# TensorE held to the planner's order, and float32 steps let in by groups

## The chip, the cores and the metric

The kernel runs on one core of one Trainium2 chip. The metric is the device time of one execution in microseconds (us). The profile shows one execution, with the engines TensorE (PE, its weight loads as PEld), VectorE (DVE), ScalarE (ACT), GpSimd (POOL) and SyncE (SP).

## The reference, cut to what matters

Two transformer blocks on 256 tokens of width 1024, in float32:

```python
def first_block(x, mem, ...):                 # two layers
    for l in range(2):
        if l == 1: k_shared, v_shared = split(rmsnorm(h, kv_norm) @ w_kv)
        main, mq = split(rmsnorm(h, norm_mix[l]) @ w_in[l])
        main_out = pool_mixer(main) if l == 0 else swa_sink_attention(norm(main), k_shared, v_shared, sinks)
        mem_out = memory_attention(norm(mq), mk, mv)        # mk, mv = mem @ w_mem_kv[l]
        h = h + concat(main_out, mem_out) @ w_out[l]
        h = h + relu(rmsnorm(h) @ w_up[l])**2 @ w_down[l]
def second_block(x, ...):
    hq, hf, hi, hg, aq, ak, av, gl = split(rmsnorm(x) @ w_in)
    y_hg = hgrn2_mix(hq, hf, hi, hg) @ w_branch_hg          # a gated linear recurrence, 8 heads
    att = moba_attention(norm(aq), norm(ak), av, bias)      # 256 tokens: causal softmax attention, 8 heads of 128
    x = x + (sigmoid(gl0) * y_hg + sigmoid(gl1) * (att @ w_branch_attn)) @ w_out
    return x + (silu(rmsnorm(x) @ w_gate) * (rmsnorm(x) @ w_up)) @ w_down
```

## The kernel before, in words

All large products are made of split operands. An activation x is kept as xh + xl and a weight as wh + wl, both halves in float32r, and each product is three matmuls (xh wh, xh wl, xl wh) into one PSUM bank. `lin` (L316) has 128 tokens as the stationary operand and 512 weight columns moving; `lin_T` (L327) has 128 weight columns stationary and 256 tokens moving. Weights stream in through the SP queue in units of two k-tiles (`load_units`, L227), and ACT and DVE make wh and wl of each. These products are the long steps here.

The rest of TensorE's work is short and in plain float32: transposes (`tr`, L158), scores, values, the pooling products and the products of the recurrence. In the trace a plain float32 matmul stands as two instructions, a transpose as one. A stage has four PSUM banks for `acc` and four for `mm`.

The order of the program is written by a planner, `Line` (L84). Each piece of work is a generator with a rank. A `yield` of a number says how long after now its next step is due; a `yield` of events waits until all are due; `Event.at(lat)` sets a due time. `mm` and `tr` move the planner's clock `now` by the time that they are taken to need. `run` (L105) takes, of all steps that are due, the one with the lowest rank. `lin` yields after every six matmuls and `lin_T` after every twelve, so that short steps can come between. Within one step nothing comes between.

What the planner writes is the program order. In the first section (L727 to L827) DVE, ACT, POOL and PE keep it. Behind that section the compiler's scheduler puts each engine's instructions in order when it builds the program: it goes by priority (the program order), models when operands will be ready, and takes a later instruction where an earlier one would have to wait.

Three stages mix short chains with long products:

- the first mixing stage (about 42 to 84 us): `pool_mix` (rank 4, L911), `mem_attention` for two token tiles (ranks 3 and 4, L861), against the second memory projection (rank 14) and `mixer_out` (ranks 20 and 21);
- the second (about 300 to 353 us): four `swa` chains (ranks 4 and 7, two at a time by `slots`, L1004), two `mem_attention` chains (ranks 3 and 6), against `in_proj` (ranks 12 and 17) and `mixer_out`;
- the third (about 550 to 800 us): `diagonal` and `recurrence` (ranks 5, 8, 9), `heads_T` (rank 9), two `attend` chains (ranks 4 and 5, L1396), against `attention_in` (rank 10) and `sides` (rank 12).

Two places hold two results in one PSUM bank and read the first before they write the second:

```python
# attend, score(hp): one acc bank for two heads                       L1407
for i in range(2):
    mm(ps[:, i, :nk], aq[tt][:, hd, :], ak[hd // 4][:, hd % 4, :nk])
    V.tensor_tensor_reduce(sc[:, i, :nk], ps[:, i, :nk], ...)
# pool_mix: one mm bank for tiles k0 and k0 + 1, three banks           L931
for k in (k0, k0 + 1):
    ... mm(ps[q0:q1, k - k0, :], pw[...], u[...], ...)
    A.activation(xh, ps[:, k - k0, :], AF.Copy, ...)
    V.scalar_tensor_tensor(xl, ps[:, k - k0, :], ..., xh, ...)
```

`swa` takes a bank for each head, and `mem_attention` issues all its score matmuls before the first read.

Of the kernel before, what the change touches and what calls it, by code (L numbers as in the profile page):

```python
# [9 lines left out]
F32R = mybir.dt.float32r  # L10
# [9 lines left out]
TT = S // P  # L20
# [21 lines left out]
def kernel(  # L42
# [8 lines left out]
    nc = tc.nc  # L51
    V, A, G, PE = nc.vector, nc.scalar, nc.gpsimd, nc.tensor

    const = ctx.enter_context(tc.tile_pool(name="const", bufs=1))
    wpool = ctx.enter_context(tc.tile_pool(name="wpool", bufs=1))
    keep = ctx.enter_context(tc.tile_pool(name="keep", bufs=1))
# [19 lines left out]
    class Event:  # L76


        t = None
# [4 lines left out]
    class Line:  # L84

        def __init__(self):
            self.now = 0.0  # L90
            self.tasks = []

        def add(self, rank, gen):
            t = [rank, 0.0, gen, None]
            self.tasks.append(t)
            return t

        def start_of(self, t):
# [6 lines left out]
        def run(self, until):  # L105
            left = list(until)
            while any(t in self.tasks for t in left):
                can = [(t, self.start_of(t)) for t in self.tasks]
                can = [(t, s) for t, s in can if s is not None]
                first = min(s for _, s in can)  # L110
                self.now = max(self.now, first)
                t = min((t for t, s in can if s <= self.now), key=lambda t: t[0])
                try:
                    y = next(t[2])
                except StopIteration:
                    self.tasks.remove(t)
                    continue
                if isinstance(y, (int, float)):
                    t[1] = self.now + y
                else:  # L120
                    t[3] = [y] if isinstance(y, Event) else list(y)

    line = Line()
# [26 lines left out]

    def mm(out_, lhsT, rhs, start=True, stop=True):
        PE.matmul(out_, lhsT, rhs, start=start, stop=stop)  # L152
        n = math.prod(rhs.shape[1:])
        m = math.prod(lhsT.shape[1:])
        side_by_side = 4 if m <= 32 else 2 if m <= 64 else 1
        line.now += max(n, min(m, 64)) / 2400.0 * (1 if rhs.dtype == F32R else 4) / side_by_side + 0.0025

    def tr(out_, in_):  # L158
        PE.transpose(out_, in_, ident)  # L159
        line.now += 0.109  # L160

    def acc_bank():
# [373 lines left out]
    def mixer_out(key, xs, cuts, there):  # L536

        left = {(tt, c): len(cuts) + 1 for tt in range(TT) for c in range(2)}

        def task(tt, k0, k1, wait):  # L540
            yield wait
            for c in range(2):
                acc = acc_bank()
                yield from lin(acc, ktiles(xs, tt)[k0:k1], W((key, k0, c)))
                left[tt, c] -= 1
                residual_ms(tt, c, acc, left[tt, c] == 0)

        return [line.add(20 + tt, task(tt, k0, k1, wait)) for tt in range(TT)
                for k0, k1, wait in zip((0,) + cuts, cuts + (KT,), there[tt])]


# [171 lines left out]
        V.tensor_sub(xs[1][:, o, :], r, xs[0][:, o, :].bitcast(F32))  # L723

    pw = act.tile([P, 6, 192], F32, tag="pw", name="pw")
    ET = mybir.EngineType
    with tc.manual_schedule(engines={ET.DVE, ET.Activation, ET.Pool, ET.PE}):  # L727

        x_raw, m_raw = raw_T(), raw_T()

        warm = mm_bank()
        for _ in range(12):
            PE.matmul(warm[:, :P], ones, ones, start=True, stop=True)

        def units_of(i, **a):
            key, w = plan[i][:2]
            ready[key] = []
            units = load_units(*w, **a)

            def more():  # L740
                ready[key] += next(units)
                return ready[key][-KU:], len(ready[key]) - KU

            return more

        def columns_T(ps, xs, w, k, c0):

            for i, (wh, wl) in enumerate(w):
                xh, xl = ktiles(xs)[k + i]
                c = slice(c0, c0 + P)  # L750
                for j, (a, b) in enumerate(((wh, xh), (wh, xl), (wl, xh))):
                    mm(ps, a[:, c], b, k + i + j == 0, k + i == KT - 1 and j == 2)

        def rows(accs, xs, w, k):
            for tt in range(TT):
                run(lin(accs[tt], ktiles(xs, tt)[k:k + KU], w, k == 0, k + KU == KT))

        load_T(x_raw, xT, 0, 2)
        ups = [acc_bank()[:, :S] for _ in range(4)]
        more = units_of(0, apart=1)  # L760
        for k in range(0, KT, KU):
            if k:
                load_T(x_raw, xT, k, 2)
            split_raw(x_raw, xs0, k, 2, G_MIX)
            w, _ = more()
            for i in range(4):
                columns_T(ups[i], xs0, w, k, i * P)
        ups += [mm_bank()[:, :S] for _ in range(2)]
        more = units_of(1)
        pool_short()  # L770
        ws = []
        for k in range(0, KT, KU):
            w, _ = more()
            ws += w
            for i in range(2):
                columns_T(ups[4 + i], xs0, w, k, i * P)
        for tt in range(TT):
            nc.sync.dma_start(h[tt], x[0, tok(tt), :])
        nc.sync.dma_start(cols, columns)
        for k in range(0, KT, 4):  # L780
            load_T(m_raw, memT, k, 4)

        dg = act.tile([P, TT, P], F32, tag="dg", name="dg")
        nx = [Norm(h[tt]) for tt in range(TT)]
        for tt in range(TT):
            for c in range(2):
                nx[tt].add(c)
            x_r[tt] = nx[tt].rstd()
            V.tensor_scalar(dg[:, tt, :], ident, x_r[tt], None, op0=ALU.mult)
        split_raw(m_raw, mem_set, 0, 4)  # L790
        qs = mm_bank().rearrange("p (t c) -> p t c", t=TT)
        rb = act.tile([P, S], F32, tag="rb", name="rb")
        more = units_of(2)

        def queries(tt):
            run(lin(qs[:, tt, :], ktiles(xs0, tt), [(wh[:, 256:], wl[:, 256:]) for wh, wl in ws]))

        queries(0)
        ps = mm_bank()[:, :S]
        for tt in range(TT):  # L800
            PE.matmul(ps[:, tok(tt)], ones, dg[:, tt, :], start=True, stop=True)
        A.copy(rb, ps)
        queries(1)
        for i in range(2):
            V.tensor_tensor(u[:, i, :], ups[i], rb, ALU.mult)
        w, k = more()
        accs1 = [acc_bank() for _ in range(2)]
        rows(accs1, mem_set, w, k)
        split_raw(m_raw, mem_set, 4, 4)
        for i in range(2, 4):  # L810
            V.tensor_tensor(u[:, i, :], ups[i], rb, ALU.mult)
        rows(accs1, mem_set, *more())
        for i in range(4, 6):
            V.tensor_tensor(u[:, i, :], ups[i], rb, ALU.mult)
        for tt in range(TT):
            A.activation(mq[tt], qs[:, tt, :], AF.Copy, scale=x_r[tt])
        m = [act.tile([P, D], F32, tag="raw_T", name="mem", bufs=4) for _ in range(TT)]
        tc.keep_in_program_order(nc.sync.dma_start(m[0], mem[0, tok(0), :]))
        rows(accs1, mem_set, *more())
        tc.keep_in_program_order(nc.sync.dma_start(m[1], mem[0, tok(1), :]))  # L820
        mem_r[0] = row_norm(m[0])
        rows(accs1, mem_set, *more())
        mem_r[1] = row_norm(m[1])
        nc.gpsimd.dma_start(pw, pool_w[0].rearrange("g a d -> (g a) d").rearrange("(j p) d -> p j d", p=P))
        for e in mem_there:
            e.at()
# [6 lines left out]
    def add_mem_kv(l, rank, lat, accs=None):  # L833
# [10 lines left out]
                A.activation(v[:, mt, :], acc[:, 256:], AF.Copy, scale=mem_r[mt])  # L844
                key_tasks.append(line.add(3, keys_T(acc, mem_r[mt], kT, mt, there[mt], lat)))

        return kT, v, there, line.add(rank, proj())

    def keys_T(acc, r, kT, tt, done, lat):

# [139 lines left out]

    act.open("mlp0")
    new_h()
    t = line.add(26, mlp("mlp0", xs, there, 8, 4, SqRelu(), residual_r))
    xs1 = xset()
    there1 = add_turned(xs1)
    line.run([t, t_bias])
# [86 lines left out]
        line.add(4, keys_T(acc, h_r[tt], skT, tt, sk_there[tt], 6.0))  # L1083

    for tt in range(TT):
        line.add(9, kv_proj(tt))
        line.add(12, in_proj("in1", 0, xs1, tt, h_r, pj, there1[tt]))
    for tt in range(TT):
        line.add(17, in_proj("in1", 1, xs1, tt, h_r, pj, there1[tt]))
    mts = xset()  # L1090
    mixed, recalled = [events() for _ in range(2)], events()

# [60 lines left out]

    t_line = line.add(2, bias_line())
    new_h()
    t = line.add(11, mlp("mlp1", xs, there, 8, 4, SqRelu(), residual_2))
    x2 = xset()
    there2, = add_norms((x2, gain(G_MIX2)))
    line.run([t, t_line])
# [154 lines left out]
                yield from to_tm("hi", c, hv, tt)  # L1314
            hv_there[tt].at(3.2)

    line.add(3, values_h())
    for c in range(2):
        line.add(3, gates_T(c))
        line.add(8 + c, recurrence(c))  # L1320


# [129 lines left out]
        done.at(3.0)  # L1452

    yat, yat_there = xset(), events()
    line.add(10, attention_in())
    for tt in range(TT):
        line.add(4 + tt, attend(tt, yat, yat_there[tt]))

# [58 lines left out]
                        residual(tt, c, accs[c])  # L1517

    new_h()
    t = line.add(12, sides())  # L1520
    xs = xset()
    there, = add_norms((xs, gain(G_FFN)))
    line.run([t])
# [8 lines left out]
        if last:  # L1532
            nc.sync.dma_start(out[0, tok(tt), cs], hs)

    line.run([line.add(26, mlp("ffn", xs, there, 11, 2, SiluGate(), finish, 2))])
    act.close()


# [49 lines left out]
```

## Time and profile before

| | |
|---|---|
| median of 3 runs | 1039.11 us (1039.04 to 1039.41) |
| the profiled execution | 1038.09 us, its span 1036.1 us |
| PE busy | 1025.5 us (99%) |
| DVE, ACT, POOL busy | 639.7 (62%), 562.8 (54%), 99.1 us (10%) |
| chain that ended last | PE 96% |

The span is from the first to the last instruction of the execution. The ends of matmuls are modelled, so that starts are read, not ends; two starts in a row give what the first one cost.

### The profile page before, as it was taken

To read this page: it belongs to the slowest core of one execution; us is meant where nothing else is said; L and a number is where in the kernel's file an instruction comes from. 1 tells how busy PE (TensorE), PEld (TensorE's weight loads), DVE (VectorE), ACT (ScalarE), POOL (GpSimd) and SP (SyncE) were. 2 spreads that over 40 slices of the span, in tenths; PEclk is the share of its full clock that TensorE was granted. 3 is DMA by queue.
4 is the path that set the end of the run, shared out by engine and by line. 5 is a ranking of instruction groups with operands and counts; after the bars stand their busy time and mean duration, and the time that the engine had idled before them with its cause. 6 is when DMAs were issued, how large, how long until landed. Compare 5 with 4: busy or idle time off the path is not lost.

```text
span 1036.1 us, 18404 instructions
## 1 busy us (share of the span) xinstructions
PE 1025.5 (99%) x7352; PEld 904.8 (87%) x7352; DVE 639.7 (62%) x1001; ACT 562.8 (54%) x901; POOL 99.1 (10%) x143
## 2 busy tenths in 40 slices
PE   8999999999999999999999999999999999999998
PEld 8768989998876788899988988888999988999997
DVE  5886655556668666464576569847635766464552
ACT  6775554454678654454465444758644555344351
POOL 1515000000143000000000004330000000000000
PEclk9999999999999999999999999999999999999999
DMA  9754556546642258656557544344365566565741
GB/s 320 269 181 136 181 184 211 191 163 204 202 164 82 57 189 317 210 185 213 173 182 235 193 165 153 119 137 145 119 203 180 169 196 210 164 211 164 234 144 41
DMA packets 107749, 186.40 MB, mean 180 GB/s; under 512 B 6792, under 2 KB 31632, under 8 KB 107664
## 3 DMA queue, kind: packets, MB, share of 16 engines
q1 hardware_dynamic: 106560, 180.43, 53.4%
q0 software_dynamic: 1104, 4.80, 1.4%
q8 instruction: 57, 0.93, 0.4%
q14 instruction: 28, 0.23, 0.1%
HBM read 182.58 MB, written 2.63 MB: 179 GB/s over the span
## 4 chain that ended last, share of the span: by engine, by line
PE 96%; DVE 1%; POOL 1%; DMA 1%; ACT 0%; issue 0%; SPq 0%; ACTq 0%
PE acc L152 59%; PE mm L152 33%; PE mm L159 3%; DMA raw<-in_w_in_dram 1%; POOL win L921 0%; DVE wl L251 0%; DVE wl L246 0%; POOL st L419 0%; POOL win L920 0%; POOL st L348 0%; ACT wh L250 0%; DVE win L921 0%; ACT wh L245 0%; ACT xh L722 0%; SPq L235 0%
## 5 line engine op out<-in xcount | busy, mean ns | idle before, releaser
L246 DVE TENSOR_TENSOR wl<-raw,wh 128x1024 fp32r<-128x1024 f32 (+1 forms) x315 | 378.1, 1223 | 172.2 <-ACT wh L245 165.6
L245 ACT CAST wh<-raw 128x1024 fp32r<-128x1024 f32 (+1 forms) x315 | 322.3, 1047 | 170.7 <-PE acc L152 101.8
L152 PE MATMUL mm<-xh,wh 128*128 128x256 f32 x752 | 208.4, 277 | 0.0
L152 PE MATMUL mm<-xl,wh 128*128 128x256 f32 x752 | 208.0, 277 | 0.0
L152 PE MATMUL mm<-xh,wl 128*128 128x256 f32 x752 | 207.9, 277 | 0.0
L152 PEld LDWEIGHTS mm<-xh,wh 128*128 128x128 f32 x752 | 141.2, 188 | 1.4 <-issue 0.4
L152 PEld LDWEIGHTS mm<-xl,wh 128*128 128x128 f32 x752 | 141.3, 188 | 1.0
L152 PEld LDWEIGHTS mm<-xh,wl 128*128 128x128 f32 x752 | 141.3, 188 | 0.0
L152 PE MATMUL acc<-wh,xh 128*128 128x512 f32 x336 | 138.3, 412 | 1.2 <-ACT wh L250 1.2
L152 PE MATMUL acc<-wh,yl 128*128 128x512 f32 x342 | 134.8, 394 | 0.0
L152 PE MATMUL acc<-wl,yh 128*128 128x512 f32 x342 | 134.0, 392 | 0.0
L152 PE MATMUL acc<-wl,xh 128*128 128x512 f32 x336 | 132.4, 394 | 1.1 <-DVE wl L251 1.1
L152 PE MATMUL acc<-wh,yh 128*128 128x512 f32 x342 | 133.4, 390 | 0.0
L152 PE MATMUL acc<-wh,xl 128*128 128x512 f32 x336 | 132.6, 395 | 0.0
L152 PE MATMUL acc<-xh,wh 128*128 128x256 f32 x416 | 117.1, 281 | 1.0 <-ACT wh L245 1.0
L152 PE MATMUL acc<-xh,wl 128*128 128x256 f32 x416 | 116.5, 280 | 1.2 <-DVE wl L246 1.2
L152 PE MATMUL acc<-xl,wh 128*128 128x256 f32 x416 | 116.2, 279 | 0.0
L152 PEld LDWEIGHTS acc<-xh,wl 128*128 128x128 f32 x416 | 78.7, 189 | 1.8 <-DVE wl L246 1.8
L152 PEld LDWEIGHTS acc<-xh,wh 128*128 128x128 f32 x416 | 78.6, 189 | 1.6 <-ACT wh L245 1.6
L152 PEld LDWEIGHTS acc<-xl,wh 128*128 128x128 f32 x416 | 78.2, 188 | 0.0
L152 PEld LDWEIGHTS acc<-wh,xh 128*128 128x128 f32 x336 | 63.2, 188 | 16.0 <-issue 2.5
L152 PEld LDWEIGHTS acc<-wl,yh 128*128 128x128 f32 x342 | 64.2, 188 | 13.7
(240 smaller groups left out, 1277.6 us busy)
## 6 DMA issues: line engine op xcount, KB each, us to landing
raw<-in_w_in_dram SPq DMA_DIRECT2D x87, 512.0 KB, 4.7
raw<-in_w_up_dram SPq DMA_DIRECT2D x64, 512.0 KB, 4.8
raw<-in_w_down_dram SPq DMA_DIRECT2D x64, 512.0 KB, 4.8
raw<-in_w_out_dram SPq DMA_DIRECT2D x24, 512.0 KB, 4.6
raw<-in_w_ffn_gate_dram SPq DMA_DIRECT2D x44, 256.0 KB, 4.3
raw<-in_w_ffn_up_dram SPq DMA_DIRECT2D x44, 256.0 KB, 4.6
raw<-in_w_ffn_down_dram SPq DMA_DIRECT2D x22, 512.0 KB, 5.3
raw<-in_w_mem_kv_dram SPq DMA_DIRECT2D x8, 512.0 KB, 9.4
```

What stands on the lines that cost most here:

```text
L152: PE.matmul(out_, lhsT, rhs, start=start, stop=stop)
L159: PE.transpose(out_, in_, ident)
L245: A.copy(wh[:, ks, :], raw[:, ks, :])
L246: V.tensor_sub(wl[:, ks, :], raw[:, ks, :], wh[:, ks, :].bitcast(F32))
```

## The change

An outer `manual_schedule` around the whole kernel makes TensorE keep the program order everywhere; the other engines are scheduled as before. Each task is marked as long (split products) or short, and the planner gets a rule, `choose`. It knows by `in_long` whether the last matmul written was a float32r one. If it was, a short step of a rank above 2 is put off as long as a long step is due and the earliest due time among the due short steps lies less than 1.6 us back. If it was not, due short steps go ahead of a long one.

```diff
+    ET = mybir.EngineType
+    ctx.enter_context(tc.manual_schedule(engines={ET.PE}))
...
+        PATIENCE = 1.6
...
+            self.in_long = True
-        def add(self, rank, gen):
-            t = [rank, 0.0, gen, None]
+        def add(self, rank, gen, long=False):
+            t = [rank, 0.0, gen, None, long]
...
+        def choose(self, ready):
+            t, _ = min(ready, key=lambda c: c[0][0])
+            longs = [c for c in ready if c[0][4]]
+            short = [c for c in ready if not c[0][4]]
+            if not longs or not short:
+                pass
+            elif self.in_long:
+                if t[0] > 2 and not t[4] and self.now - min(s for _, s in short) < self.PATIENCE:
+                    t = min(longs, key=lambda c: c[0][0])[0]
+            elif t[4]:
+                t = min(short, key=lambda c: c[0][0])[0]
+            return t
...
-                t = min((t for t, s in can if s <= self.now), key=lambda t: t[0])
+                t = self.choose([(t, s) for t, s in can if s <= self.now])
...
         PE.matmul(out_, lhsT, rhs, start=start, stop=stop)
+        line.in_long = rhs.dtype == F32R
...
         PE.transpose(out_, in_, ident)
+        line.in_long = False
...
-        return [line.add(20 + tt, task(tt, k0, k1, wait)) for tt in range(TT)
+        return [line.add(20 + tt, task(tt, k0, k1, wait), True) for tt in range(TT)
...
-    with tc.manual_schedule(engines={ET.DVE, ET.Activation, ET.Pool, ET.PE}):
+    with tc.manual_schedule(engines={ET.DVE, ET.Activation, ET.Pool}):
...
-    line.add(10, attention_in())
+    line.add(10, attention_in(), True)
```

The same mark `True` goes to the other tasks of long products: the memory projection, `kv_proj`, both `in_proj`, the three `mlp`, `values_h`, `gates_T` and `sides`.

## Rows read from the trace of the kernel before

**Rows 1.** The page: busy time of the engines, share of span.

```profile
PE 1025.5 (99%) x7352; PEld 904.8 (87%) x7352; DVE 639.7 (62%) x1001; ACT 562.8 (54%) x901; POOL 99.1 (10%) x143
```

**Rows 2.** Busy time by stretch: two mixing stages; length, engines, granted clock, DMA.

```profile
52.90:84.00 31.10, 30.18 (x161) 19.79 (x160) 22.79 (x54) 18.72 (x44) 9.68 (x13) 1.00 0.48 150
302.60:352.80 50.20, 50.18 (x327) 34.40 (x326) 35.65 (x132) 35.78 (x106) 13.82 (x36) 1.00 0.23 71
```

**Rows 3.** Timeline of PE, second mixing stage: start, length, instruction, shape, count.

```profile
302.60 0.49 PE L159 MATMUL mm<-ident,qn 128*128 128x128 f32 x3
302.84 0.48 PE L152 MATMUL acc<-wh,xh 128*128 128x512 f32 x1
303.15 0.39 PE L152 MATMUL acc<-wl,xh 128*128 128x512 f32 x1
...
304.07 0.40 PE L152 MATMUL acc<-wh,xl 128*128 128x512 f32 x1
304.39 0.49 PE L152 MATMUL acc<-skT,qT 64*128 64x128 f32 x4
304.81 0.50 PE L152 MATMUL acc<-wh,xh 128*128 128x512 f32 x1
305.15 0.39 PE L152 MATMUL acc<-wl,xh 128*128 128x512 f32 x1
305.38 0.39 PE L152 MATMUL acc<-wh,xl 128*128 128x512 f32 x1
...
350.74 0.66 PE L152 MATMUL mm<-eT,sv 128*64 128x128 f32 x8
```

**Rows 4.** Timeline of PE and DVE, the first scores of `attend`.

```profile
705.19 0.82 PE L152 MATMUL acc<-ak,aq 128*128 128x128 f32 x4
...
705.71 0.29 DVE L1411 CUSTOM_DVE_ANT_0 sc<-acc,rel 128x128 f32<-128x128 f32 x1 [1.64 <-PE acc L152]
...
706.07 0.47 PE L152 MATMUL acc<-ak,aq 128*128 128x128 f32 x2
706.15 0.42 DVE L1411 CUSTOM_DVE_ANT_0 sc<-acc,rel 128x256 f32<-128x256 f32 x1
...
706.64 0.70 PE L152 MATMUL acc<-ak,aq 128*128 128x256 f32 x2
```

**Rows 5.** Timeline of PE and DVE, a later score of `attend`.

```profile
711.08 0.39 PE L152 MATMUL acc<-ak,aq 128*128 128x128 f32 x2
...
713.88 0.29 DVE L1411 CUSTOM_DVE_ANT_0 sc<-acc,rel 128x128 f32<-128x128 f32 x1
...
714.73 0.38 PE L152 MATMUL acc<-ak,aq 128*128 128x128 f32 x2
```

**Rows 6.** Timeline, first mixing stage: the pooling products and their readers.

```profile
53.43 1.86 PE L152 MATMUL mm<-u,pw 128*128 128x256 f32 x8
...
55.61 0.85 ACT L941 ACTIVATE xh<-mm,cols 128x256 fp32r<-128x256 f32 x2
...
58.70 1.22 PE L152 MATMUL mm<-u,pw 64*64 64x256 f32 x4 [0.92 <-DVE u L926]
...
61.35 0.48 DVE L942 SCALAR_TENSOR_TENSOR xl<-mm,cols,xh 128x256 fp32r<-128x256 f32 x1
```

**Rows 7.** Timeline of PE: memory attention's scores (mkT) and turned softmax (me).

```profile
56.08 1.13 PE L152 MATMUL acc<-mkT,mqT 64*128 64x256 f32 x8
...
68.97 0.60 PE L159 MATMUL mm<-ident,me 128*128 128x128 f32 x4
...
331.53 1.14 PE L152 MATMUL acc<-mkT,mqT 64*128 64x256 f32 x8
...
336.61 0.60 PE L159 MATMUL mm<-ident,me 128*128 128x128 f32 x4
```

**Rows 8.** Timeline: the recurrence's last products, and the first later use of their result.

```profile
682.55 0.39 PE L152 MATMUL mm<-hv,AX 128*128 128x128 f32 x2
...
713.27 0.69 DVE L1482 TENSOR_TENSOR ho<-ho,hgate 128x512 f32<-128x512 f32 x1
```

More of the change, by code (lines that the diff above doesn't have):

```diff
@@ L725 @@
     pw = act.tile([P, 6, 192], F32, tag="pw", name="pw")
-    ET = mybir.EngineType
-    with tc.manual_schedule(engines={ET.DVE, ET.Activation, ET.Pool, ET.PE}):
+    with tc.manual_schedule(engines={ET.DVE, ET.Activation, ET.Pool}):
         x_raw, m_raw = raw_T(), raw_T()
@@ L845, in proj @@
                 key_tasks.append(line.add(3, keys_T(acc, mem_r[mt], kT, mt, there[mt], lat)))
-        return kT, v, there, line.add(rank, proj())
+        return kT, v, there, line.add(rank, proj(), True)
     def keys_T(acc, r, kT, tt, done, lat):
@@ L992 @@
     new_h()
-    t = line.add(26, mlp("mlp0", xs, there, 8, 4, SqRelu(), residual_r))
+    t = line.add(26, mlp("mlp0", xs, there, 8, 4, SqRelu(), residual_r), True)
     xs1 = xset()
@@ L1085 @@
     for tt in range(TT):
-        line.add(9, kv_proj(tt))
-        line.add(12, in_proj("in1", 0, xs1, tt, h_r, pj, there1[tt]))
+        line.add(9, kv_proj(tt), True)
+        line.add(12, in_proj("in1", 0, xs1, tt, h_r, pj, there1[tt]), True)
     for tt in range(TT):
-        line.add(17, in_proj("in1", 1, xs1, tt, h_r, pj, there1[tt]))
+        line.add(17, in_proj("in1", 1, xs1, tt, h_r, pj, there1[tt]), True)
     mts = xset()
@@ L1155 @@
     new_h()
-    t = line.add(11, mlp("mlp1", xs, there, 8, 4, SqRelu(), residual_2))
+    t = line.add(11, mlp("mlp1", xs, there, 8, 4, SqRelu(), residual_2), True)
     x2 = xset()
@@ L1315, in values_h @@
             hv_there[tt].at(3.2)
-    line.add(3, values_h())
+    line.add(3, values_h(), True)
     for c in range(2):
-        line.add(3, gates_T(c))
+        line.add(3, gates_T(c), True)
         line.add(8 + c, recurrence(c))
@@ L1519 @@
     new_h()
-    t = line.add(12, sides())
+    t = line.add(12, sides(), True)
     xs = xset()
@@ L1533, in finish @@
             nc.sync.dma_start(out[0, tok(tt), cs], hs)
-    line.run([line.add(26, mlp("ffn", xs, there, 11, 2, SiluGate(), finish, 2))])
+    line.run([line.add(26, mlp("ffn", xs, there, 11, 2, SiluGate(), finish, 2), True)])
     act.close()
```

## The prediction

> **What bounds the kernel now.** The page's first part comes first: TensorE is busy 99% of the span and the next engine 62% [rows 1]. A time can thus change in three ways only: TensorE gets other matmuls (it does not, the products are the same), a matmul costs another pitch, or TensorE stands. The busy share can't show which, as the modelled ends cover short waits. So I read starts in the timeline. Two wide long matmuls in a row start 0.23 us apart (305.15, 305.38), and stretches of long products alone run at that pitch from end to end; nothing is to be had there, and the planner writes them in one order with or without the rule. What is left are the stages that mix. By the windows, two of them last 31.1 and 50.2 us [rows 2], with DVE at 73% and 71% and ACT at 60% and 71%, so that the chains compete there for DVE and ACT with the making of wh and wl.
>
> **What a change between long and short costs.** Three transposes and the long one behind them take 302.60 to 303.15, 0.55 us; less 0.23 that is 0.107 us for each transpose, and nothing for the change [rows 3]. Four score instructions on half the rows of the array (64*128) are another matter: from the last long one before (304.07) to the second behind (305.15) pass 1.08 us; less two pitches, 0.62 us. Two side-by-side pairs at 0.11 (a pair streams as many columns as a transpose) would need 0.22, so this group pays 0.40 us for changing to and fro [rows 3]. I count 15 groups with such half-array forms between long ones in the second stage, from 304.39 to 350.74 [rows 3], and take half as many, 8, in the first (an estimate). Transposes, the scores of `attend` and its values use the whole array: by the first reading they pay nothing.
>
> [...]
>
> **The change part by part.**
>
> *Grouping.* A short step is now put off by 1.6 us of planner time, and since it can enter only after a long step of six matmuls (1.3 us), by 1.6 to 2.9 us; those that fall due meanwhile go with it. Saved at most: all 15 + 8 groups at 0.40, 9.2 us; at least nothing. Chains fall due at scattered moments and at most four run at once, so I let about a third, 7.5 groups, merge: **-3 us**. In the recurrence the two halves already go together, so nothing merges there. Each of its levels becomes due some 2 us later; over seven levels the chain ends some 12 us later. What hides that: its last product starts at 682.55 and the result is first used at 713.27 [rows 8], 30 us later; beyond that margin every us would count.
>
> *Order kept: the scores of `attend`.* Before, the scheduler puts something between the two heads of one bank: the other tile's head and a long matmul. The rows show why: TensorE issues the first halves of both tiles at 705.19, DVE reads the first tile's at 705.71, and the second half starts at 706.07, right behind the read; the other tile's read starts at 706.15 and takes 0.42, and its second half starts at 706.64 [rows 4]. In program order head 0, its read and head 1 are one step, so TensorE stands in between, and the long products queue behind it. Price with DVE free: a first half of two instructions at 0.11 leaves TensorE free at 705.41, so 0.66 us until 706.07; the wider one leaves at 705.85 (two of 0.22 behind it), so 0.79 until 706.64. Two tiles by four calls: 4 x 0.66 + 4 x 0.79 = 5.8 us at least. With DVE taken by something else it is much more: at 711.08 a first half is issued, free at 711.30, but DVE reads it only at 713.88 and is done at 714.17 [rows 5], a wait of 2.9 us. Half of the calls like that and half free would make 4 x 2.9 + 4 x 0.72 = 14.5. I take six at 0.72 and two halfway (1.8): **+8 us**, nearer the lower end, because a TensorE that stands asks for fewer wh and wl meanwhile.
>
> *Order kept: `pool_mix`.* The same in three banks, with two readers in a row: the score's wait less its read, 0.66 - 0.29 = 0.37, plus ACT 0.43 (0.85 for two), plus DVE 0.48 [rows 6] and one more hand-over of 0.07 (706.00 to 706.07 in rows 4): 1.35 us a bank, 4.1 for three. Upper bound: the first half of the first bank is issued at 53.43 and its xl starts at 61.35 [rows 6], 7.9 us, because DVE makes the windows and wl first; with two free banks 10.6. Of this 0.92 is already paid (TensorE idle before 58.70 [rows 6]). Lower bound, where these waits only replace what the stage loses to DVE anyway: nothing. I take 4.1 + 1 for DVE's queue - 0.9: **+4 us**.
>
> *Order kept: the softmax of `mem_attention`.* The planner makes its transposes due 3.2 us behind the scores. The trace has 12.9 us (56.08 to 68.97) in the first stage and 5.1 (331.53 to 336.61) in the second [rows 7]. With patience the distance becomes 4.8 to 6.1. In the second stage that is enough; in the first up to 12.9 - 4.8 = 8 us can be exposed, once, though much of that distance is TensorE's own pooling work. Between 0 and 8: **+2 us**.
>
> *Long work used up.* Long steps that go ahead of due shorts in the second stage are missing later, when only chains are left. The half of `in_proj` that fills there is 48 matmuls, 11 us. If it ends early, TensorE stands in the gaps of two chains at a time; I bound this by 0 and 6 (about half the filler) and take **+1 us**.
>
> Nothing moves on the SP or POOL queues; no DMA is issued by TensorE. The first section already kept this order.
>
> Sum: -3 + 8 + 4 + 2 + 1 = +12 us. Against the profiled execution, 1038.09 us (1036.1 span and 2.0 around it), that is 1050; the median of the runs is 1.0 higher, so 1051.
>
> **The rivals.**
>
> *Not slower: grouping outweighs the waits.* The place is the two mixing stages. It decides where merged groups x 0.40 exceed the new waits. If nearly all 23 merge (-9.2) and the first stage is bound by DVE in either order (pooling and softmax waits 0), what stays is the scores' 5.8: -3.4, 1035.7. For it: DVE at 73% in that stretch, and a wait already there. Against: 5.8 comes from rows with DVE free, and chains of seven steps can't all fall together. Chance 0.14.
>
> *No change that shows.* Merges save 8 or so and only the floor of the waits is paid, within 2 us of zero: 1039. It needs the planner's due times to lie behind the real ones nearly everywhere, as they do where stages are calm. Chance 0.13.
>
> *Waits compound.* If the planner is early throughout, each stall delays the reads behind it and the stage goes at the pace of the chains: scores 14.5, pooling 9.7, softmax 8, filler 6, grouping -3, +35 at the top; halfway between that and the forecast is +23, 1062. For it: the distances of rows 5 to 7. Against: in those the scheduler had given DVE other work because nothing pressed. Chance 0.20.
>
> *The forecast.* Chance 0.53, with its own range of 1044 to 1058 (scores 6 to 11, pooling 1 to 7, the rest as above).
>
> **How the numbers follow.** 0.2% is 2 us, about what a measurement can tell here. Faster by more: 0.14 from the first rival. Same: 0.13. Slower: 0.53 + 0.20 = 0.73. The range leaves out most of the first rival below and the upper half of the third above, 0.1 each: 1037 to 1064.
>
> **What the profile after would show.** Right: the two heads' instructions of one tile stand next to each other in `attend`, with PE starts 0.9 us or more apart and waits of PE on DVE L1411 in the view of waits, eight of them, 6 to 11 us in all, between about 700 and 760; waits of PE on DVE L942 in the first mixing stage; fewer groups of half-array forms in the second (about 10 for 15), each longer; long stretches as before at 0.23. Wrong: no PE wait on L1411, or the third stage no longer than now; the second stage shortened by more than 5 us (grouping worth more than I give it); or the time moved in a stretch of long products, where I see nothing to move.

## The result, and the profile after

The changed kernel takes 1068.68 us (median of 4 runs, 1067.32 to 1070.12), the kernel before 1039.22 beside it: a ratio of 1.0283 [1.0267, 1.0299], 29.5 us slower. Slower was forecast, by 12 us; the time lies above the range that went up to 1064.

First the page of the kernel after: busy time by engine, TensorE's granted clock over 40 slices of the span, and the chain that ended last. They answer to [rows 1].

```profile
PE 1030.0 (97%) x7352; PEld 908.6 (85%) x7352; DVE 642.7 (60%) x1001; ACT 564.0 (53%) x901; POOL 103.4 (10%) x143
...
PEclk9989999999998999999999999999899999999999
...
PE 92%; DVE 3%; ACT 2%; issue 1%; DMA 1%; POOL 1%; SPq 0%; DVEq 0%; ACTq 0%
```

The instruction counts are the same, and the busy share is again useless: it fell by two points for 29.8 us of span. What is new is that the chain leaves TensorE for DVE and ACT, and that three slices of the clock read 8. So the next view is the one of waits (engine and line that waited, what for; us in total, times, longest).

```profile
PE acc L173 <- DVE s L1433: 9.4, 8, 5.2
PE mm L173 <- DVE xl L964: 7.7, 3, 5.5
PE mm L173 <- ACT eT L471: 3.6, 3, 2.3
PE acc L173 <- ACT qT L1044: 3.6, 1, 3.6
```

L1433, L964 and L173 are L1411, L942 and L152 of the kernel before. None of these four rows is in its view of waits. The eight waits of the first row are the scores of `attend`, the three of the second the pooling, and the four of the last two rows belong to the short chains, three of them in the second stage.

Where the time went is read from landmarks that both traces have, the turnings of `h` and `xn` between the stages. The first stage runs from the start to the first turned `h` (88.1 us before, 96.0 after), the second from the eighth to the last of the twelve `ident,h` groups (281.1 to 367.9; 289.1 to 383.9), the third from the last `ident,xn` ahead of the recurrence to the next one (550.7 to 845.0; 566.6 to 874.5). They last 8.0, 8.0 and 13.6 us longer; between them nothing moved by more than 0.4.

The first mixing stage, in the timeline of TensorE and DVE:

```profile
55.36 1.22 PE L173 MATMUL mm<-u,pw 128*128 128x256 f32 x4
...
60.40 1.21 DVE L269 TENSOR_TENSOR wl<-raw,wh 128x1024 fp32r<-128x1024 f32 x1
61.53 0.16 DVE L451 TENSOR_SCALAR hs<-hs 128x4 f32<-128x4 f32 x1
61.60 0.48 DVE L964 SCALAR_TENSOR_TENSOR xl<-mm,cols,xh 128x256 fp32r<-128x256 f32 x1
...
62.13 3.21 PE L173 MATMUL mm<-u,pw 128*64 128x256 f32 x8 [5.54 <-DVE xl L964]
```

The products of the first half of the first bank are issued at 55.36, but DVE makes windows and four wl (one is shown) before it reads that half at 61.60 (0.48 us, so until 62.08), and the second half starts at 62.13, right behind that read. In the program order nothing stands in between: TensorE waits 5.54 us. [Rows 6] had the same late read, at 61.35, behind other work of TensorE.

The second mixing stage, in the timeline of TensorE, ACT and DVE, where one group of short instructions goes from 320.10 to the long product at 345.85:

```profile
319.78 0.40 PE L173 MATMUL acc<-wh,xl 128*128 128x512 f32 x1
320.10 1.13 PE L173 MATMUL acc<-mkT,mqT 64*128 64x256 f32 x8
320.21 0.69 ACT L688 ACTIVATE pj<-acc,st 128x512 f32<-128x512 f32 x1 [0.32 <-PE acc L173]
...
326.30 1.23 PE L173 MATMUL acc<-skT,qT 64*128 64x256 f32 x4 [3.64 <-ACT qT L1044]
...
339.49 1.09 PE L173 MATMUL mm<-eT,mv 128*64 128x128 f32 x16 [2.29 <-ACT eT L471]
...
342.40 0.88 DVE L394 TENSOR_TENSOR xl<-mm,xh 128x256 fp32r<-128x256 f32 x2
...
345.85 0.47 PE L173 MATMUL acc<-wh,xh 128*128 128x512 f32 x1
...
347.50 0.69 DVE L484 TENSOR_TENSOR h<-acc,h 128x512 f32<-128x512 f32 x1 [0.85 <-PE acc L173]
```

That is 25.7 us without one long product, because until after 342 none was to be had. The product at 319.78 is the last of the 144 of `kv_proj` and `in_proj`, and the `pj` at 320.21 takes out their last result. The next long products belong to `mixer_out`, whose results go into `h` from 347.50 on; it multiplies what the chains make, and the first of that is ready after 342.40. In the kernel before, the last `in_proj` product stands among the chains at 321.30, 40.2 us into the stage (30.7 in the kernel after), and the first one of `mixer_out` follows 5.4 us later:

```profile
321.30 0.47 PE L152 MATMUL acc<-wh,xl 128*128 128x512 f32 x1
...
326.72 0.48 PE L152 MATMUL acc<-wh,xh 128*128 128x512 f32 x1
```

In the third stage seven of the eight waits between two heads last 0.39 to 0.90 us, 4.2 in all. The eighth, with DVE and ACT beside it:

```profile
748.33 2.60 DVE L269 TENSOR_TENSOR wl<-raw,wh 128x1024 fp32r<-128x1024 f32 x2 [0.15 <-ACT wh L268]
...
749.04 0.39 PE L173 MATMUL acc<-ak,aq 128*128 128x128 f32 x2
...
749.68 1.28 ACT L1502 ACT_TABLE_LOAD   x1
750.98 1.08 ACT L1502 ACTIVATE hgate<-acc 128x512 f32<-128x512 f32 x2
...
751.68 1.29 DVE L1503 TENSOR_TENSOR hgate<-acc,hgate 128x512 f32<-128x512 f32 x2 [0.76 <-ACT hgate L1502]
752.88 1.28 DVE L1504 TENSOR_TENSOR ho<-ho,hgate 128x512 f32<-128x512 f32 x2
754.31 0.29 DVE L1433 CUSTOM_DVE_ANT_0 sc<-acc,rel 128x128 f32<-128x128 f32 x1
...
754.66 0.80 PE L173 MATMUL acc<-ak,aq 128*128 128x128 f32 x2 [5.24 <-DVE s L1433]
```

The reader of the score stands on DVE behind two wl and behind the gates' products, which wait for ACT (0.76 us), and ACT loads a table first (1.28 us). TensorE pays for all of it: 5.24 us.

### The profile page after: what moved, and what is told of

The parts are those of the page before. It is cut to its first block, busy times and chain, and to the rows that moved or that the text cites. A ratio compares the mean times of both kernels' runs of the same rounds, so it can differ in the third digit from the quotient of the medians.

```text
span 1065.9 us, 18406 instructions
## 1 busy us (share of the span) xinstructions
PE 1030.0 (97%) x7352; PEld 908.6 (85%) x7352; DVE 642.7 (60%) x1001; ACT 564.0 (53%) x901; POOL 103.4 (10%) x143
## 4 chain that ended last, share of the span: by engine, by line
PE 92%; DVE 3%; ACT 2%; issue 1%; DMA 1%; POOL 1%; SPq 0%; DVEq 0%; ACTq 0%
PE acc L173 56%; PE mm L173 32%; PE mm L181 3%; DMA raw<-in_w_in_dram 1%; ACT me L911 1%; POOL win L943 0%; DVE wl L274 0%; DMA raw<-in_w_out_dram 0%; DVE wl L269 0%; ACT wh L268 0%; ACT sc L1060 0%; ACT L1502 0%; DVE win L943 0%; DVE sc L1433 0%; POOL st L442 0%
## 5 line engine op out<-in xcount | busy, mean ns | idle before, releaser
L173 PE MATMUL mm<-xh,wh 128*128 128x256 f32 x752 | 208.2, 277 | 0.0
L173 PE MATMUL mm<-xl,wh 128*128 128x256 f32 x752 | 207.8, 276 | 0.0
L173 PE MATMUL mm<-xh,wl 128*128 128x256 f32 x752 | 207.8, 276 | 0.0
L173 PEld LDWEIGHTS mm<-xh,wh 128*128 128x128 f32 x752 | 141.2, 188 | 1.4 <-issue 0.4
L173 PEld LDWEIGHTS mm<-xl,wh 128*128 128x128 f32 x752 | 141.3, 188 | 1.0
L173 PEld LDWEIGHTS mm<-xh,wl 128*128 128x128 f32 x752 | 141.3, 188 | 0.0
L173 PE MATMUL acc<-wh,xh 128*128 128x512 f32 x336 | 135.5, 403 | 1.2 <-ACT wh L273 1.2
L173 PE MATMUL acc<-wh,yl 128*128 128x512 f32 x342 | 134.7, 394 | 0.0
L173 PE MATMUL acc<-wl,yh 128*128 128x512 f32 x342 | 134.0, 392 | 0.0
L173 PE MATMUL acc<-wh,yh 128*128 128x512 f32 x342 | 133.4, 390 | 0.0
L173 PE MATMUL acc<-wl,xh 128*128 128x512 f32 x336 | 131.6, 392 | 1.1 <-DVE wl L274 1.1
L173 PE MATMUL acc<-wh,xl 128*128 128x512 f32 x336 | 131.9, 393 | 0.0
L173 PE MATMUL acc<-xh,wh 128*128 128x256 f32 x416 | 116.7, 281 | 0.9 <-ACT wh L268 0.8
L173 PE MATMUL acc<-xh,wl 128*128 128x256 f32 x416 | 116.4, 280 | 1.2 <-DVE wl L269 1.2
L173 PE MATMUL acc<-xl,wh 128*128 128x256 f32 x416 | 116.1, 279 | 0.0
L173 PEld LDWEIGHTS acc<-xh,wl 128*128 128x128 f32 x416 | 78.7, 189 | 1.8 <-DVE wl L269 1.8
L173 PEld LDWEIGHTS acc<-xh,wh 128*128 128x128 f32 x416 | 78.5, 189 | 1.4 <-ACT wh L268 1.3
L173 PEld LDWEIGHTS acc<-xl,wh 128*128 128x128 f32 x416 | 78.1, 188 | 0.1
L173 PEld LDWEIGHTS acc<-wl,yh 128*128 128x128 f32 x342 | 64.2, 188 | 13.7
L173 PEld LDWEIGHTS acc<-wl,xh 128*128 128x128 f32 x336 | 63.2, 188 | 14.8 <-DVE wl L274 2.3
```

## The experiments

Theory "order": the fixed order costs the time, through waits inside steps (two halves of one bank with a reader between them) and through steps whose data come later than the planner thinks. Rival "rule": the grouping itself makes the chains late. The stages are measured by the landmarks above, each over before's (88.1, 86.8 and 294.3 us), from one profiled execution each. A fall of the granted clock is in such a number too: the third stage has the same order of TensorE's instructions in `repaired_no_rule_in_second` as in `both_repaired` and stands at +3.4 for +1.6, with the clock at half for 3.4 us from 627.5 on. "Over before" is the difference of the medians measured together.

| kernel | median us | over before | ratio, 95% | 1st | 2nd | 3rd |
|---|---|---|---|---|---|---|
| the change | 1068.68 | +29.5 | 1.0267 to 1.0299 | +8.0 | +8.0 | +13.6 |
| order_alone | 1067.30 | +28.6 | 1.0258 to 1.0289 | +14.0 | +3.2 | +12.5 |
| rule_alone | 1043.46 | +4.7 | 1.0034 to 1.0065 | -1.1 | +4.7 | +1.2 |
| scores_first | 1056.86 | +18.1 | 1.0158 to 1.0188 | +7.0 | +7.9 | +1.4 |
| pool_banks | 1062.10 | +23.4 | 1.0207 to 1.0244 | +3.3 | +7.7 | +13.6 |
| both_repaired | 1050.32 | +11.8 | 1.0088 to 1.0125 | +2.7 | +7.4 | +1.6 |
| repaired_no_rule_in_second | 1045.67 | +7.1 | 1.0033 to 1.0075 | +1.8 | +3.2 | +3.4 |
| order_repaired_no_rule | 1046.48 | +7.0 | 1.0048 to 1.0079 | +5.5 | +1.8 | +0.6 |
| filled_wait | 1067.92 | +29.4 | 1.0242 to 1.0318 | +7.2 | +7.1 | +11.8 |
| rule_in_first_and_third | 1038.01 | -0.5 | 0.9984 to 1.0005 | +2.1 | 0.0 | +0.7 |
| repairs_alone | 1039.14 | -0.4 | 0.9986 to 1.0005 | +1.1 | +0.1 | +0.4 |

**The two parts by themselves.** `order_alone` keeps TensorE's program order and takes the due step of lowest rank, as before; `rule_alone` has the rule, and the scheduler places TensorE's instructions.

```diff
# order_alone, in choose()
             t, _ = min(ready, key=lambda c: c[0][0])
-            longs = [c for c in ready if c[0][4]]
...
             return t
# rule_alone
-    ctx.enter_context(tc.manual_schedule(engines={ET.PE}))
...
-    with tc.manual_schedule(engines={ET.DVE, ET.Activation, ET.Pool}):
+    with tc.manual_schedule(engines={ET.DVE, ET.Activation, ET.Pool, ET.PE}):
```

> TensorE keeps the program order, but the planner chooses by rank alone as before. Theory 'order': what costs is that TensorE can no longer step past a wait inside a step or an early due time; the scores of attend and the pooling products wait as in the changed kernel, so most of the +29.5 us stays: 1056 to 1068 us, with at least two stretches at half clock. Rival 'rule': the delay of short steps by 1.6 us is what empties TensorE later; without it the program order is near what the scheduler made of it: 1039 to 1046 us.

> The planner's new rule, but TensorE scheduled as before. Theory 'order': the scheduler steps past the waits again, and the grouping gives or takes little: 1035 to 1043 us, clock 1.00 throughout. Rival 'rule': the chains are late and long work runs out in the second mixing stage, 1048 to 1062 us.

The order alone costs 28.6 us, within the interval the same as the whole change; the rule alone costs 4.7, about all of it in the second stage, a little more than theory "order" had allowed (up to 1043) and with the clock at half there for 6.8 us, where 1.00 throughout was expected. The order is the larger part by far. The two kernels with the fixed order differ by stage: with the rule the first stage is 6.0 us shorter and the second 4.8 longer. The first of these is not shown to be the rule's: `order_alone` is at half clock there for some 20 us, the change for some 7.

**The waits inside the steps.** `scores_first` writes the scores of both heads of a step before it reads either; `pool_banks` gives each pooling tile a PSUM bank of its own; `both_repaired` does both.

```diff
# scores_first, in attend's score()
                 mm(ps[:, i, :nk], aq[tt][:, hd, :], ak[hd // 4][:, hd % 4, :nk])
+            for i in range(2):
+                hd = 2 * hp + i
+                c = slice(hd, hd + 1)
                 V.tensor_tensor_reduce(sc[:, i, :nk], ps[:, i, :nk], ...
# pool_banks
-            ps = mm_bank().rearrange("p (k t) -> p k t", t=S)
             for k in (k0, k0 + 1):
+                ps = mm_bank()[:, :S]
...
```

> The changed kernel, with both score matmuls of attend's step ahead of both reads of the bank (one bank as before). Theory 'order': the waits on the first read vanish, 9 to 12 us come back in the third mixing stage, the half clock near 755 us goes with them: 1057 to 1060 us. Rival 'rule': the waits come from the chains' due times and move to the next step: 1065 to 1069 us.

> The changed kernel, with a PSUM bank for each of the six pooling tiles in place of one for two. Theory 'order': the 5.5 us wait for xl at the first bank and two of 1.1 us go, and with them the half clock near 62 us: 5 to 8 us less, 1061 to 1064 us. Rival 'the stage is bound by VectorE': TensorE waits as long at the next step (the softmax, the third bank's u): within 2 us of 1068.7.

> The changed kernel with both repairs, the score matmuls ahead of the reads and a bank for each pooling tile. Theory 'order', each wait pays for itself: the gains of the two repairs add up (11.8 and 6.6 us), 1050 us, and what is left, 11 us over the kernel before, lies in the second mixing stage (8) and the first. Rival 'one pays for the other': they share the half clock or the filler, 1054 us or more.

They take back 11.3 and 6.1 us (29.5 less 18.1, 29.5 less 23.4), and 17.7 together. `scores_first` does so in the third stage, where 12.2 of 13.6 us go, and `pool_banks` in the first. Most of what is left is in the second stage. The view of waits of `both_repaired` has neither xl nor the scores' s any more; it begins:

```profile
PE mm L173 <- ACT eT L471: 3.8, 3, 2.5
PE acc L173 <- ACT qT L1044: 3.6, 1, 3.6
PE mm L181 <- DVE me L475: 2.0, 1, 2.0
```

The two heads use different columns of one bank, and yet TensorE waited for the reader of the other columns, eight times of eight in the kernel after (9.4 us in all); with the reads behind both products no such wait is left in `scores_first` or `both_repaired`. Why a read of other columns holds the second product back is not shown.

**The rule without those waits.** `repaired_no_rule_in_second` is `both_repaired` with the rule off in the second mixing stage; `order_repaired_no_rule` has both repairs and the rule nowhere.

```diff
# repaired_no_rule_in_second
             t, _ = min(ready, key=lambda c: c[0][0])
+            if not self.rule:
+                return t
...
     act.open("mix1")
+    line.rule = False
...
     act.open("mlp1")
+    line.rule = True
```

> Both repairs, and the delay of short steps switched off in the second mixing stage alone. Theory 'long work used up': the rule costs 5 us there whether TensorE is ordered or not, since its due steps wait while the fillers go: 1045 to 1047 us, and fewer than 5 us at half clock there. Rival 'the order alone costs there': no change beyond 1.5 us against both repairs, about 1050.

> The fixed order with both repairs (the scores of attend read after both heads' products, a PSUM bank for each pooling tile) and without the rule: the planner writes the due step of lowest rank, as before. Theory order (the fixed order costs through waits inside steps and through due times that are early; the rule gains nothing): the repairs give what they gave with the rule, 18.4 us, so 1067.3 - 18.4 = 1049, a ratio near 1.010, no slower than the 1050.3 with the rule. Rival, the rule pays once the waits inside the steps are gone: without it at least 3 us slower than with it, 1053 or more.

Without the rule in the second stage 4.7 us go (11.8 to 7.1), and without it anywhere 4.8: with the waits repaired, the rule costs in the second stage and earns nothing that shows in the sum. Why it costs can be read from all the traces. In the six kernels with the rule on in this stage the last product of `in_proj` starts 30.7 us into the stage, and the next long one comes 21.0 (`rule_alone`) to 26.1 us later; in the six without it the last one starts 40.2 to 42.9 us into the stage, and the next comes 5.4 to 6.8 later. The rule lets the long products go first and so uses up the filler; then the chains stand alone.

The order left by itself costs 7.0 us (1046.5 where 1049 was expected: without the rule the repairs took back 21.6 us, not 18.4). 5.5 of them are in the first stage, where the clock is at half for 13.5 us (last section). In its second stage the clock is full and TensorE is busy 91.75 of 94.0 us (windows: length, busy time of PE, PEld, DVE, ACT, POOL, granted clock, share and GB/s of DMA):

```profile
281.00:375.00 94.00, 91.75 (x523) 68.81 (x523) 68.52 (x186) 67.10 (x164) 22.95 (x44) 1.00 0.41 126
```

`order_alone` has the same order of TensorE's instructions in this stage, but its clock is at half for one stretch in which TensorE is busy throughout, and its stage takes 90.0 us for 88.6. So 3.4 us at half clock cost 1.4 where TensorE had work:

```profile
330.30:333.65 3.35, 3.35 (x14) 2.19 (x13) 2.19 (x9) 2.59 (x7) 0.22 (x1) 0.50 0.04 15
```

Where nothing stands between the heads their scores cost little: in `order_repaired_no_rule` the first eight score instructions, both tiles, go in one piece from 713.36, and the next long product starts 1.13 us later.

**The clock.** In the second stage of the kernel after, the clock falls to half within the 3.64 us wait (rows in the last section). `filled_wait` puts 28 instructions that do no work of the kernel into that wait.

```diff
# filled_wait, in mem_attention behind its transposes
+        if l == 1 and tt == 1:
+            warm = mm_bank()
+            for _ in range(14):
+                PE.matmul(warm[:, :P], ones, ones, start=True, stop=True)
```

> The changed kernel with 28 idle matmul instructions (ones times ones into a bank of its own, no use made of them; 3.1 us at 0.11) in TensorE's wait of 3.64 us in the second mixing stage, behind the transposes of the second tile's memory queries. Theory 'the half clock costs': the granted clock stays at 1.00 there and the 10 us of short steps behind the wait go faster, 1064 to 1067 us. Rival 'the chains set the pace': clock 1.00 or not, DVE and ACT take as long, 1068 to 1070 us.

The times are too scattered to tell (1064.4 to 1073.4); the longer ones have the lower mean granted clock (0.990 in the two shortest, 0.985 and 0.981 in the others). The profiled execution is the shortest. Timeline, then windows:

```profile
321.76 3.29 PE L893 MATMUL mm<-ones 128*128 128x128 f32 x28
325.57 0.70 PE L173 MATMUL acc<-skT,qT 64*128 64x256 f32 x4 [0.52 <-ACT qT L1048]
...
331.83 0.70 PE L173 MATMUL acc<-skT,qT 64*128 64x256 f32 x4
335.85 1.98 PE L173 MATMUL mm<-eT,mv 128*64 128x128 f32 x16 [3.31 <-ACT eT L471]
```

```profile
325.10:335.00 9.90, 6.97 (x50) 4.17 (x50) 8.57 (x40) 7.80 (x27) 4.15 (x7) 1.00 0.16 49
335.20:341.80 6.60, 5.96 (x40) 4.66 (x40) 3.36 (x15) 4.54 (x16) 0.00 (x0) 0.50 0.00 0
```

The clock stays at 1.00, and the scores that started at 336.50 in the kernel after start at 331.83 (3.9 us sooner within the stage). But the next product then waits 3.31 us for ACT instead of 2.29, the clock falls after all, at 335.1, and the stage ends only 0.8 us sooner (94.0 for 94.8). So the half clock was put off and shortened, from 10.2 to 6.8 us, not removed. The longer wait shows that the chains hold TensorE back there; what the stage would take at full clock throughout is not shown.

**Can either part pay under the scheduler?** `rule_in_first_and_third`, against its label, is `rule_alone` with the rule off from the second mixing stage to the end, so in the first alone (`line.rule = False` at `act.open("mix1")`); `repairs_alone` is the kernel before with both repairs.

> TensorE scheduled as before, the new rule on in the first mixing stage and off from the second on (not switched on again). Theory 'long work used up': the 4.8 us of the rule alone came from the second stage; without it there the first stage's 1 us stays as a gain: 1037 to 1039 us. Rival 'the rule costs everywhere': 1041 to 1043 us.

> The kernel before, its scheduler placing TensorE's instructions, with both repairs alone. Theory order: there the scheduler already puts other products between a bank's first half and its second, so the repairs have nothing to remove: within 2 us of before, 1037 to 1040, ratio 0.998 to 1.001. Rival, the shared banks cost time in either order: faster by 3 us or more, 1035.5 or less.

Both are the same as before within 0.2%. In the views of waits of the kernel before and of `repairs_alone` TensorE has no row on the scores' s or the pooling's xl, so the repairs have nothing to take away there: they mend what the fixed order broke. No version here beats the kernel before.

## Why the prediction was off

**The order's waits: mechanism right, sizes too small.** The place, the line and the count were as said: eight waits on the reader of the scores, three on xl. The scores were sized +8 us (5.8 to 14.5) and cost 11.3. Seven of the eight waits came out at 0.60 us on average, a little under the 0.66 and 0.79 taken; "two halfway (1.8)" was one at 5.24, nearly twice the 2.9 of [rows 5], because the reader stood behind another chain in DVE's queue. Pooling was sized +4 (0 to 9.7) and cost 6.1: 5.54 us at one bank for the "1 for DVE's queue". The prediction had seen this late read in [rows 6] and kept it as the upper end; for this bank it was the nearer one, since DVE reads it about as late in both kernels (61.35 and 61.60).

**Softmax: not seen in the changed kernel.** Its view of waits has no row on me. With the pooling repaired a wait of 2.0 us on me appears in the first stage; that it has the size of the +2 predicted says little, since it does not show where the pooling's waits stand.

**Grouping and "long work used up": this step failed, by its size.** Together they were -2 us, about -1 in the second stage, which lost 8.0. Grouping did happen there: the groups with half-array forms went from 15 to 7, which saves at most 3.2 us by the 0.40 of [rows 3], and the prediction's guess of a third was too low. "Long work used up" had the mechanism: long steps go ahead of due short ones and are missing later. But it was taken at +1 and bounded by 6, about half the filler, as if the filler might end a little early. It ended 9.5 us earlier in the stage (30.7 for 40.2), `mixer_out` could not start before the chains had made its operands, and for 25.7 us TensorE went at the pace of ACT and DVE, which make each link's data (waits of 3.64 and 2.29 us in the rows). The scheduler could not help: `rule_alone` has such a stretch of 21.0 us with a wait of 3.42 us on the same qT. That the rule is the cause of some 4.7 us of the 8.0 is shown by three comparisons (`rule_alone` 4.7, `repaired_no_rule_in_second` 4.7, `order_repaired_no_rule` 4.8); how the 4.7 divides between the chains' waits and the clock, which is at half for 6.8 to 10.2 us in this stage with the rule and for 3.4 or less without, was not separated. The other 3.3 us are the order's (`order_alone` 3.2), for which the prediction had no term in this stage.

**The sum by stages.** Forecast about +5, -1 and +8 (the grouping's -3 shared by its 8 and 15 groups); measured +8.0, +8.0 and +13.6. Of 17.5 us missing, 9 are the second stage. The rival "waits compound" had the size (up to +35) and, with a stage at the pace of the chains, part of the mechanism, at a chance of 0.20; its objection, that before DVE was late only where nothing pressed, did not hold: in the kernel after DVE reads at 61.60 and 754.31 while TensorE stands.

**Right by its own tests.** The long stretches kept their pitch (0.23 us for 512 columns in both kernels), and no product waits for the recurrence's result. "The third stage no longer than now" would have refuted the step, and it is 13.6 longer. The half clock was in none of its steps.

## What to carry to other kernels

Before fixing the order of an engine that is never idle, look for steps in which it writes, another engine reads and it writes again into the same bank: here the scheduler hid those readers, and the fixed order exposed each of them for as long as the reader's queue was, not only the read (at the longest 5.24 us for a read of 0.29). A rule that puts short steps off also uses up the filler that hid the chains; count the long products that do not depend on the chains, and price the chains' latency from where these end, stage by stage. And a repair is worth something only where the wait exists: the same two edits gave 17.7 us in the fixed order and nothing under the scheduler.

## What the hardware showed that was not expected

TensorE's granted clock fell to half (0.50 in the windows) in each of the three stages that waited. Windows of the kernel after (columns as above):

```profile
58.95:65.65 6.70, 3.52 (x10) 1.25 (x12) 5.81 (x7) 1.32 (x2) 1.83 (x2) 0.50 0.91 293
325.15:335.25 10.10, 8.95 (x36) 5.00 (x36) 6.62 (x31) 6.75 (x24) 3.49 (x5) 0.50 0.21 57
751.85:758.55 6.70, 3.89 (x16) 3.49 (x16) 3.56 (x11) 3.29 (x8) 0.00 (x0) 0.50 0.42 145
```

Each begins within one of the three longest waits (5.54, 3.64 and 5.24 us); in [rows 2] the clock is 1.00. With the waits on scores gone, the stretch near 752 is at 1.00 (window 748 to 758 of `scores_first`). In `order_repaired_no_rule` the fall comes within a wait of 2.10 us on xl, before 61.69, and the clock stays at half for 13.5 us, in which long products start 0.43 us apart (72.95, 73.38, 73.81) for 0.23 after it (75.07, 75.30):

```profile
61.00:74.50 13.50, 11.87 (x35) 6.70 (x36) 8.00 (x24) 5.21 (x17) 1.62 (x2) 0.50 0.41 132
```

What it costs is bounded by the rows: TensorE was busy 16.4 us in the three stretches of the kernel after (3.52 + 8.95 + 3.89), so at full clock at most half of that, 8.2 us, could have been saved, by this estimate. In `order_repaired_no_rule` the same estimate gives up to 5.9 us (half of 11.87), most of the 7.0 that this kernel is over before. `filled_wait` ended its stage 0.8 us sooner with 3.4 us less at half clock, and the pair of `order_alone` and `order_repaired_no_rule` shows 1.4 us for 3.4.

How much of each stage's loss is the clock's was not separated.
